# Two hidden tiles of the first network: gate tiles plain by block, input tiles as the first seven-product pair

## The chip, the cores and the metric

The kernel runs on one core of one Trainium2 chip. The metric is the device time of one execution in microseconds (us). Of the kernel before, three runs gave 2673.63, 2676.51 and 2676.99 us; the median is 2676.51 us.

## What is computed

One step of one decoder layer on 1032 tokens (1024 of a prompt and 8 samples), with 1024 features: a gated network, a mixer, a second gated network and a gated input embedding, each with a residual and a layer norm. The change is in the first network:

```python
def swiglu(x, wi, wo):
    g, u = jnp.split(x @ wi, 2, axis=-1)
    return (jax.nn.silu(g) * u) @ wo

x = layer_norm(ALPHA * x + 0.5 * swiglu(x, ffn1_wi, ffn1_wo), ln_g[0], ln_b[0])
```

`wi` has 2 x 2816 columns: 22 tiles of 128 gate columns (`g`) and 22 tiles of 128 input columns (`u`). The second network has the same form with weights of its own.

## The kernel before

**Precision.** Every float32 operand of a matrix product is split into a high part (a rounding copy on ACT) and a low part (a subtraction on DVE): `hilo` for activations (L211, L212), `wload` for plain weight tiles (L148, L149), `wcomb` for combined weight tiles (L258, L259). A product is then three matmuls: high x high, high x low, low x high.

**Tokens.** The tokens lie in four blocks of 256, 260, 256 and 260 columns (`BLK4`). Blocks 0 and 2 belong to half s = 0, blocks 1 and 3 to half s = 1.

**Plain tiles.** `unit` (L169 to L175) multiplies one weight tile of 1024 x 128 with one block: 8 row tiles times 3, which is 24 matmuls. Over four blocks one tile costs 96 matmuls.

**Pairs.** `pair` (L438 to L482, its matmuls in `product`, L432 to L434) computes two weight tiles at once over all four blocks by a scheme of seven products instead of eight: 7 products x 2 halves x 12 matmuls = 168, where two plain tiles take 192. It needs seven combinations of the weights (`wcomb`, L249 to L278) and of the blocks (`xsums`, L219 to L227, called four times, `kp` = 0 to 3, for each half). One call of `xsums` takes four `tmp` tiles, of which there are four in all, two subtractions on DVE (L222, L224), two on POOL (L223, L225), then four copies on ACT (L211) and four subtractions on DVE (L212). The call for half 0 of all `kp` runs in `xlate`; those for half 1 stand beside the first four steps of the first pair (`late_sums`, `beside`). The first pair of a network takes products 0 and 1 of both halves first, since these need no sums, then products 2 to 6 of half 0, then those of half 1.

**The first network.** `ffn` computes hidden tiles 0 and 1 plainly: as each of the blocks 0, 2, 1, 3 arrives, `plain` multiplies it with two gate tiles (k = 0) and two input tiles (k = 1). The eight weight transfers of these four tiles (`wearly`, L533) stand ahead of the prompt's blocks 2, 1 and 3 (`xload`, L292) on SP's queue. Then come 20 pairs: for p = 1 to 10 the gate pair (k = 0) and the input pair (k = 1). `hidden` says what becomes of a result: for k = 0 it is written to the tile `sg` and put through Silu; for k = 1 it is written to a `tmp` tile and multiplied into `sg` (L499). `wi_raw` loads the columns of a pair (L245) into two of four slots in turn; slots 30 and 31 also hold a part of block 2, and slots 32 and 33 two of the eight tiles of the transposed x (`rows1`).

**Order.** The engines run their instructions in order; the order on each is made by a scheduler when the program is built. Weight tiles go round a ring of nine slots (`RING`), and results in PSUM round `mm` (four buffers), `pn` (every fifth plain result) and `aux` (three).

Of the kernel before, what the change touches and what calls it, by code (L numbers as in the profile page):

```python
# [8 lines left out]
F32 = mybir.dt.float32  # L9
# [13 lines left out]
NHID = FF // 128  # L23
# [40 lines left out]
def layer_kernel(ctx: ExitStack, tc: tile.TileContext, I, O):  # L64
# [4 lines left out]
    rawp = ctx.enter_context(tc.tile_pool(name="raw", bufs=3))  # L69
# [7 lines left out]
    def gen(i, dt=F32, n=NT):  # L77

        tag = f"a{i}" if isinstance(i, int) else i
        return sb.tile([128, 1024 if tag in WN else 4 * BM], dt, name=tag, tag=tag)[:, :1024 if tag in WN else n]  # L80
# [403 lines left out]
    def ffn(wi, wo, l, XS, enter, xlate, raws, sgs, RTs, res, groups, plains, tail, extra=None):  # L484
# [3 lines left out]
        def hidden(k, ws, sg, first):  # L488


            def out(i, c, fn):
                d = bs(sg[i], c, BLK4)
                if k == 0:
                    fn(d)
                    S.activation(d, d, AF.Silu)
                else:
                    t = tmp(BN[c % 2])
                    fn(t)
                    V.scalar_tensor_tensor(d, d, 0.5, t, op0=OP.mult, op1=OP.mult)  # L499

            pair(ws, XS, (0, 1), out, first)
# [18 lines left out]
            DQ.dma_start(hsum[5, p], sg[0][:, h[1]])  # L520

        def wi_raw(p, k):
            i = 2 * p + k
            return wraw(wi, k * FF + p * 256, raws[2 * (i % 2):2 * (i % 2) + 2])

        tail_slots = dict(sum(plains, []))
        sg = [gen(sgs[i]) for i in range(2)]
        wp, first = [], []
# [21 lines left out]
        def plain(c):  # L550
            if early and not wp:
                halves(c)
            for k in range(2):
                for i in range(2):
                    if len(wp) < 4:
                        wp.append(wcol(wi, k * FF + i * 128, raws=early.pop(0) if early else ()))
                    if first:
                        ps = first.pop(0)
                    else:
                        ps = unit_ps(BLK4[c][1])  # L560
                        unit(ps, wp[2 * k + i], [xplain(XS[c % 2], c, m) for m in range(8)])
                    d = bs(sg[i], c, BLK4)
                    if k == 0:
                        S.activation(d, ps, AF.Silu)
                    else:
                        with tc.high_priority():
                            V.scalar_tensor_tensor(d, d, 0.5, ps, op0=OP.mult, op1=OP.mult)
                        DQ.dma_start(bs(hscr[i], c, BLK4), d)

        enter(plain, wearly)  # L570
        sreg()
        wr = wi_raw(1, 0)
        with tc.issue_after(order_["entered"]) if l else nullcontext():
            w0 = wcomb(wr)
            xlate()
        for p in range(1, NHID // 2):
            for k in range(2):
                w = w0 if p == 1 and k == 0 else wcomb(wi_raw(p, k))
                if k == 0 and p > 1:
                    sg = [gen(sgs[2 * ((p + 1) % 2) + i]) for i in range(2)]  # L580
                hidden(k, w, sg, p == 1 and k == 0)
            spill(p, sg)

        def split_load(t, src):

# [85 lines left out]

    def enter1(plain, wearly):
        ts = {0: [gen(i)[:, :D] for i in (16, 17)]}
        wt = [t[:, o:o + 512] for t in [gen(i) for i in (22, 10, 24)] for o in (0, 512)]
        wt += [rawp.tile([128, 512], F32, name="raw", tag="raw") for _ in range(2)]
        st = gen(18)[:, :D]
        DQ.dma_start(st[0:8], I["x_sample"][:, 0, :])
        for i in range(2):
            xload(0, ts[0], i * 512, i * 512 + 512)
            for q in range(2):  # L680
                wearly(q, 4 * i, wt[2 * i + q])
        for i in range(4, 8):
            wearly(i // 2, i % 2 * 4, wt[i])
        warm(WARM[0])
        ps = aux()
        for m in range(8):
            T.transpose(ps[:, m * 8:(m + 1) * 8], st[0:8, m * 128:(m + 1) * 128], ident[:8, :8])
        V.tensor_copy(xsv, ps[:, 0:64])
        rows1.extend(gen(i) for i in (19, 23, 32, 33, 11, 25, 34, 35))
        parts = {0: [(0, 0, 1), (1, 4, 5)], 2: [(7, 30, 31), (6, 26, 27)],  # L690
                 1: [(0, 2, 3), (1, 6, 7)], 3: [(7, None, None), (6, 28, 29)]}
        tslots = {2: [20, 21], 1: [8, 9], 3: [12, 13]}
        prev, sr = None, sreg(R)
        for c in (0, 2, 1, 3):
            if c:
                with tc.issue_after(order_["early"]):
                    ts[c] = xtiles(c, tslots[c])
            for j, *ss in parts[c]:
                for q in range(2):
                    xset(X1[c % 2], j, q, ss[q] if ss[q] is not None else sr[:, q * 4 * BM:(q + 1) * 4 * BM])  # L700
            xinput(c, ts[c], rows1)
            xsplit(X1[c % 2], rows1, c)
            if prev is not None:
                plain(prev)
            prev = c
        plain(prev)
        parameters()
        for m in range(8):
            DQ.dma_start(xscr[m], rows1[m])
# [1121 lines left out]
```

## Time and profile before

| | us |
|---|---|
| median of three runs | 2676.51 |
| the profiled execution, whole | 2676.36 |
| its span | 2674.6 |
| PE busy | 2635.3 |
| DVE busy | 1840.7 |
| ACT busy | 1272.1 |
| POOL busy | 650.9 |

The span is the time from the first to the last instruction that the profiler shows; the execution took 1.8 us more. PE is the matrix engine, DVE, ACT and POOL the three others, SP the one that issues most transfers. A busy PE does not say that its matmuls follow one another at the closest spacing, because a matmul of about 0.28 us overlaps the next ones; how far apart they start is read from the timeline. A row of the timeline shows the start in us, the length in us, the engine, the line of the kernel, the operation with its output and input names, and in brackets how long the engine was idle before and what ended that. A row of the windows shows a stretch and its length, then for each engine asked for its busy time and number of instructions, then PE's granted clock, the share of the DMA engines and GB/s.

### The profile page before, as it was taken

The page shows a single profiled execution, that of the slowest core. Times are in us where ns is not written, and L with a number is a line of the kernel's source. Part 1 is how long each engine was busy: PE and PEld are TensorE (multiplying, and loading weights), DVE is VectorE, ACT ScalarE, POOL GpSimd, SP SyncE. Part 2 cuts the span into 40 slices and gives each one's busy share as a digit, 9 for nine tenths or more (in the row PEclk, how much of TensorE's full clock was granted, in tenths as well). Part 3 has the DMA queues.
Part 4 walks back from the last instruction along what each step waited for, and adds up shares of the span by engine and source line. Part 5 has one row for each costly group of instructions (what it writes and reads, how often), then busy time and mean ns, then how long its engine had stood idle before and what let it go on. Part 6 is the DMA issues. An engine that isn't in the chain of part 4 may idle for free.

```text
span 2674.6 us, 56234 instructions
## 1 busy us (share of the span) xinstructions
PE 2635.3 (99%) x21775; PEld 2597.2 (97%) x21775; DVE 1840.7 (69%) x4053; ACT 1272.1 (48%) x2774; POOL 650.9 (24%) x649
## 2 busy tenths in 40 slices
PE   9999999999999999999999999999999999999998
PEld 9999999999999999999999999999999999999888
DVE  6755556987885747555555678658855555888887
ACT  5544445433654444445566555426544444533351
POOL 2222221112431111111110335323322222111454
PEclk9999999999999999999999999999999999999999
DMA  6333235532233334336667676821423323643211
GB/s 208 104 108 102 89 108 185 180 121 68 88 116 96 116 100 125 90 90 191 197 193 240 220 245 210 258 80 51 155 88 108 107 87 107 219 148 117 86 51 58
DMA packets 311924, 355.15 MB, mean 133 GB/s; under 512 B 28536, under 2 KB 246344, under 8 KB 311656
## 3 DMA queue, kind: packets, MB, share of 16 engines
q1 hardware_dynamic: 289336, 330.30, 38.9%
q10 hardware_dynamic: 22320, 21.26, 2.7%
q8 instruction: 170, 2.79, 0.4%
q14 instruction: 98, 0.80, 0.1%
HBM read 246.09 MB, written 105.42 MB: 131 GB/s over the span
## 4 chain that ended last, share of the span: by engine, by line
PE 85%; DVE 7%; DMA 4%; issue 2%; ACT 2%; POOL 1%; SPq 0%; DVEq 0%; ACTq 0%; POOLq 0%
PE mm L432 15%; PE mm L433 14%; PE mm L434 14%; PE aux L432 6%; PE aux L434 6%; PE aux L433 6%; PE mm L172 5%; PE mm L174 5%; PE mm L173 5%; PE pn L172 1%; PE pn L174 1%; PE pn L173 1%; DVE a L212 1%; DVE a L589 1%; DVE a L612 1%
## 5 line engine op out<-in xcount | busy, mean ns | idle before, releaser
L432 PE MATMUL mm<-a,w 128*128 128x260 f32 (+1 forms) x2313 | 655.7, 284 | 3.0 <-DVE a L612 2.5
L433 PE MATMUL mm<-a,w 128*128 128x260 f32 (+1 forms) x2313 | 651.1, 282 | 0.9 <-DVE a L212 0.8
L434 PE MATMUL mm<-a,w 128*128 128x260 f32 (+1 forms) x2313 | 650.1, 281 | 0.0
L432 PEld LDWEIGHTS mm<-a,w 128*128 128x128 f32 x2313 | 435.3, 188 | 11.8 <-issue 8.7
L433 PEld LDWEIGHTS mm<-a,w 128*128 128x128 f32 x2313 | 435.7, 188 | 1.4 <-DVE a L212 1.3
L434 PEld LDWEIGHTS mm<-a,w 128*128 128x128 f32 x2313 | 435.3, 188 | 0.9 <-issue 0.8
L275 POOL TENSOR_TENSOR raw<-a,raw 128x512 f32<-128x512 f32 (+2 forms) x98 | 123.7, 1263 | 1137.4 <-issue 626.8
L259 DVE TENSOR_TENSOR w<-raw,w 128x512 fp32r<-128x512 f32 (+2 forms) x258 | 174.7, 679 | 198.2 <-ACT w L258 196.2
L432 PE MATMUL aux<-a,w 128*128 128x260 f32 (+1 forms) x1000 | 282.2, 282 | 0.2 <-DVE a L612 0.2
L434 PE MATMUL aux<-a,w 128*128 128x260 f32 (+1 forms) x1000 | 281.2, 281 | 0.0
L433 PE MATMUL aux<-a,w 128*128 128x260 f32 (+1 forms) x1000 | 281.1, 281 | 0.0
L432 PE MATMUL mm<-a,e 128*128 128x260 f32 (+1 forms) x785 | 222.4, 283 | 0.9 <-DVE a L612 0.9
L433 PE MATMUL mm<-a,e 128*128 128x260 f32 (+1 forms) x785 | 221.1, 282 | 1.1 <-DVE a L212 1.1
L434 PE MATMUL mm<-a,e 128*128 128x260 f32 (+1 forms) x785 | 220.9, 281 | 0.0
L174 PE MATMUL mm<-a,w 128*128 128x256 f32 (+3 forms) x739 | 208.1, 284 | 0.0
L172 PE MATMUL mm<-a,w 128*128 128x260 f32 (+4 forms) x695 | 198.5, 287 | 2.9 <-DVE a L647 1.7
L258 ACT CAST w<-a 128x512 fp32r<-128x512 f32 (+2 forms) x200 | 117.5, 588 | 171.4 <-PE mm L434 101.7
L173 PE MATMUL mm<-a,w 128*128 128x260 f32 (+4 forms) x695 | 197.4, 285 | 0.0
L432 PEld LDWEIGHTS aux<-a,w 128*128 128x128 f32 x1000 | 188.2, 188 | 2.6 <-issue 2.1
L433 PEld LDWEIGHTS aux<-a,w 128*128 128x128 f32 x1000 | 188.3, 188 | 0.0
L434 PEld LDWEIGHTS aux<-a,w 128*128 128x128 f32 x1000 | 188.2, 188 | 0.0
L258 ACT CAST w<-raw 128x512 fp32r<-128x512 f32 (+2 forms) x258 | 152.2, 591 | 67.2 <-PE aux L434 21.1
(543 smaller groups left out, 7645.9 us busy)
## 6 DMA issues: line engine op xcount, KB each, us to landing
a<-in_ffn_wi_dram SPq DMA_DIRECT2D x80, 512.0 KB
a<-in_w_in_dram SPq DMA_DIRECT2D x68, 512.0 KB
a<-hsum SPq DMA_DIRECT2D x119, 258.0 KB
hsum<-a SPq DMA_DIRECT2D x68, 258.0 KB
a<-in_ffn_wo_dram SPq DMA_DIRECT2D x40, 384.0 KB
a<-in_state_C_dram ACTq DMA_DIRECT2D x32, 256.0 KB
out_dram<-a ACTq DMA_DIRECT2D x32, 256.0 KB
raw<-in_w_b_dram SPq DMA_DIRECT2D x32, 256.0 KB
```

Source lines behind the costliest of these rows:

```text
L172: T.matmul(ps, wh, xh, start=(i == 0), stop=False)
L173: T.matmul(ps, wh, xl, start=False, stop=False)
L174: last = T.matmul(ps, wl, xh, start=False, stop=(i == n - 1))
L212: order_["lo"] = V.tensor_tensor(dst[1], src, F_(dst[0]), op=OP.subtract).ins
L258: S.copy(hi, src)
L259: V.tensor_tensor(lo, src, F_(hi), op=OP.subtract)
L275: G.tensor_tensor(s4, a12, s2, op=OP.subtract)
L432: T.matmul(ps, wh, xh, start=start and kp == 0, stop=False, skip_group_check=True)
L433: T.matmul(ps, wh, xl, start=False, stop=False, skip_group_check=True)
L434: T.matmul(ps, wl, xh, start=False, stop=stop and kp == len(xs) - 1, skip_group_check=True)
L589: V.tensor_tensor(lo, F_(lo), F_(hi), op=OP.subtract)
L612: V.tensor_tensor(r, r, ps, op=op)
```

## The change

In the first network (`l` = 0) only the gate tiles of hidden tiles 0 and 1 are computed plainly. Their input tiles (p = 0, k = 1) become the first of 21 pairs. So four early weight transfers of 256 KB fall away, and the pair loads its two of 512 KB through `wi_raw`, into slots 30 and 31. The results of the first pair now go through `tmp` and L499 into `sg`, and the pair (1, 0) gets a new pair of `sg` tiles. The two hidden tiles are stored whole by `spill`, where before each block was stored by itself (L568). The second network is as before.

```diff
         def wi_raw(p, k):
-            i = 2 * p + k
+            i = 2 * p + k + 1 - bool(l)
             return wraw(wi, k * FF + p * 256, raws[2 * (i % 2):2 * (i % 2) + 2])
...
-            for k in range(2):
+            for k in range(2 if l else 1):
                 for i in range(2):
-                    if len(wp) < 4:
+                    if len(wp) < 2 * k + i + 1:
                         wp.append(wcol(wi, k * FF + i * 128, raws=early.pop(0) if early else ()))
...
         enter(plain, wearly)
         sreg()
-        wr = wi_raw(1, 0)
+        todo = [(p, k) for p in range(NHID // 2) for k in range(2)][2 if l else 1:]
+        wr = wi_raw(*todo[0])
         with tc.issue_after(order_["entered"]) if l else nullcontext():
             w0 = wcomb(wr)
             xlate()
-        for p in range(1, NHID // 2):
-            for k in range(2):
-                w = w0 if p == 1 and k == 0 else wcomb(wi_raw(p, k))
-                if k == 0 and p > 1:
-                    sg = [gen(sgs[2 * ((p + 1) % 2) + i]) for i in range(2)]
-                hidden(k, w, sg, p == 1 and k == 0)
-            spill(p, sg)
+        for i, (p, k) in enumerate(todo):
+            w = wcomb(wi_raw(p, k)) if i else w0
+            if k == 0 and i:
+                sg = [gen(sgs[2 * ((p + bool(l)) % 2) + q]) for q in range(2)]
+            hidden(k, w, sg, i == 0)
+            if k:
+                spill(p, sg)
...
     def enter1(plain, wearly):
         ts = {0: [gen(i)[:, :D] for i in (16, 17)]}
-        wt = [t[:, o:o + 512] for t in [gen(i) for i in (22, 10, 24)] for o in (0, 512)]
-        wt += [rawp.tile([128, 512], F32, name="raw", tag="raw") for _ in range(2)]
+        wt = [t[:, o:o + 512] for t in [gen(i) for i in (22, 10)] for o in (0, 512)]
...
             for q in range(2):
                 wearly(q, 4 * i, wt[2 * i + q])
-        for i in range(4, 8):
-            wearly(i // 2, i % 2 * 4, wt[i])
```

**On SP's queue, at the start of the program.** Rows show the line, the transfer with output and input, and its shape. Before, the block 0 (`a_95`, `a_96`) and eight weight pieces stand ahead of the first tiles of block 2 (`a_191`, `a_192`):

```order
L292 DMA a_96<-in_x_prompt_dram 128x512
L533 DMA a_98<-in_ffn_wi_dram 128x4x128 x2
L533 DMA a_99<-in_ffn_wi_dram 128x4x128 x2
L533 DMA raw<-in_ffn_wi_dram 128x4x128 x2
L292 DMA a_191<-in_x_prompt_dram 128x1024
L292 DMA a_192<-in_x_prompt_dram 128x1024
```

Of the change, with block 2 in `a_184` and `a_185`:

```order
L292 DMA a_96<-in_x_prompt_dram 128x512
L533 DMA a_98<-in_ffn_wi_dram 128x4x128 x2
L292 DMA a_184<-in_x_prompt_dram 128x1024
L292 DMA a_185<-in_x_prompt_dram 128x1024
L292 DMA a_300<-in_x_prompt_dram 128x1024
```

Four transfers are gone from the place ahead of the prompt's tiles.

**On DVE, where the sums of half 1 end.** Before: the last call of `xsums` (L222, L224 and the L212 rows on `a_1015` to `a_1018`), beside the first pair, which writes its results straight to `sg` (`a_94`):

```order
L222 TENSOR_TENSOR tmp<-a_133 128x260
L212 TENSOR_TENSOR a_1015<-tmp,a_1015 128x260
L212 TENSOR_TENSOR a_1016<-tmp,a_1016 128x260
L224 TENSOR_TENSOR tmp<-a_137,tmp 128x260
L212 TENSOR_TENSOR a_1017<-tmp,a_1017 128x260
L212 TENSOR_TENSOR a_1018<-tmp,a_1018 128x260
L259 TENSOR_TENSOR w_1215<-a_1208,w_1215 128x512
L212 TENSOR_TENSOR a_1015<-tmp,a_1015 128x260
L212 TENSOR_TENSOR a_1016<-tmp,a_1016 128x260
L469 SCALAR_TENSOR_TENSOR a_94<-sreg,mm 128x256
```

Of the change, with the same sums in `a_781` to `a_784`:

```order
L222 TENSOR_TENSOR tmp<-a_126 128x260
L499 SCALAR_TENSOR_TENSOR a_93<-a_93,tmp 128x260
L212 TENSOR_TENSOR a_782<-tmp,a_782 128x260
L224 TENSOR_TENSOR tmp<-a_130,tmp 128x260
L212 TENSOR_TENSOR a_783<-tmp,a_783 128x260
L259 TENSOR_TENSOR w_990<-a_983,w_990 128x512
L212 TENSOR_TENSOR a_784<-tmp,a_784 128x260
L469 SCALAR_TENSOR_TENSOR tmp<-sreg,mm 128x256
L212 TENSOR_TENSOR a_781<-tmp,a_781 128x260
L212 TENSOR_TENSOR a_782<-tmp,a_782 128x260
```

The pair's own results (L469, L499) now go through `tmp` tiles and stand among the sums.

**On PE, where these sums are used.** Before, the last matmuls that need the low parts of `a_1015` and `a_1016`, behind product 6 of half 0 (`w_861`):

```order
L434 MATMUL mm<-a_198,w_861 128x256
L433 MATMUL mm<-a_1015,w_847 128x260
L434 MATMUL mm<-a_1015,w_847 128x260
L433 MATMUL aux<-a_1016,w_850 128x260
L434 MATMUL aux<-a_1016,w_850 128x260
L432 MATMUL aux<-a_1016,w_850 128x260
```

Of the change, with `a_781` and `a_782`, and behind them the next pair's first matmul (`w_990`):

```order
L432 MATMUL aux<-a_782,e_615 128x260
L434 MATMUL mm<-a_783,e_618 128x260
L433 MATMUL mm<-a_781,w_612 128x260
L434 MATMUL mm<-a_781,w_612 128x260
L433 MATMUL aux<-a_782,e_615 128x260
L434 MATMUL aux<-a_782,e_615 128x260
L432 MATMUL mm<-a_132,w_990 128x256
```

The low parts of the last sums stand 15 matmuls later in the pair than before: 140 of its matmuls come ahead of the first of these four rows, where 125 did.

## The prediction

> **What bounds the kernel now.** I read the page first, then the windows over the start.
>
> ```profile
> PE 2635.3 (99%) x21775; PEld 2597.2 (97%) x21775; DVE 1840.7 (69%) x4053; ACT 1272.1 (48%) x2774; POOL 650.9 (24%) x649
> PE 85%; DVE 7%; DMA 4%; issue 2%; ACT 2%; POOL 1%; SPq 0%; DVEq 0%; ACTq 0%; POOLq 0%
> 10.70:62.50 51.80, 51.80 (x436) 51.80 (x435) 35.55 (x78) 31.49 (x90) 10.74 (x11) 1.00 0.60 210
> 62.50:82.50 20.00, 20.00 (x171) 20.00 (x170) 18.25 (x38) 13.07 (x35) 8.08 (x9) 1.00 0.27 85
> 65.60:77.50 11.90, 11.90 (x103) 11.90 (x102) 11.90 (x25) 8.00 (x22) 6.46 (x7) 1.00 0.28 90
> ```
>
> The first row gives each engine's busy time, the second the chain that ended last: PE holds it. The windows (busy PE, PEld, DVE, ACT, POOL) show that PE never stops between 10.7 and 82.5 us, so a matmul removed there is time removed. But the third window has DVE at 11.90 of 11.90: while the sums of x for half 1 are made, **DVE has no room either**. The change takes work from PE ahead of just this stretch.
>
> **What goes.** Four tile-blocks of two input tiles are 2 x 4 x 24 = 192 matmuls; a pair is 168. So 24 matmuls go. Their spacing, from the timeline:
>
> ```profile
> 10.71 0.56 PE L172 MATMUL mm<-a,w 128*128 128x256 f32 x1
> 12.33 0.27 PE L174 MATMUL mm<-a,w 128*128 128x256 f32 x1
> 14.32 0.28 PE L172 MATMUL mm<-a,cd 128*128 128x256 f32 x1
> 19.87 1.15 PE L308 MATMUL aux<-ident,a 128*128 128x128 f32 x9
> 62.52 0.36 PE L432 MATMUL mm<-a,e 128*128 128x256 f32 x1
> 77.42 0.28 PE L433 MATMUL mm<-a,w 128*128 128x260 f32 x1
> 85.46 0.28 PE L432 MATMUL aux<-a,e 128*128 128x256 f32 x1
> ```
>
> The first pair begins at 62.52; the row at 85.46 is 192 matmuls later, so one takes 22.94 / 192 = 0.1195 us (not the 0.28 us that each is in flight). **Saving: 24 x 0.1195 = 2.87 us**, if PE stays busy. That is already less than 0.2% of the time (5.35 us), about what a measurement of this kernel can tell from no change.
>
> **When PE would want the sums.** Without the 192 plain matmuls PE would begin the pair 22.94 us earlier, at 39.6. The last low parts of the sums are wanted after 140 matmuls of the pair: 39.6 + 140 x 0.1195 = 56.3. Before it was 62.52 + 125 x 0.1195 = 77.46, and PE's row is at 77.42. DVE's last sum came in the same moment:
>
> ```profile
> 41.70 0.69 DVE L267 TENSOR_TENSOR raw<-a,a 128x512 f32<-128x512 f32 x1 [1.96 <-DMA a<-in_ffn_wi_dram]
> 76.78 0.76 DVE L212 TENSOR_TENSOR a<-tmp,a 128x260 fp32r<-128x260 f32 x2
> ```
>
> Its two rows end at 77.54 (76.78 + 0.76). There was no slack, and PE now comes 21.1 us earlier. Can DVE?
>
> **When DVE can begin.** The chain starts with transfers:
>
> ```profile
> 13.79 0.33 SPq L329 DMA_DIRECT2D tmp<-in_b_in_dram  x1
> 14.64 0.30 SPq L330 DMA_DIRECT2D tmp<-in_b_in_dram  x1
> 15.91 0.31 SPq L332 DMA_DIRECT2D tmp<-in_ln_g_dram  x1
> 17.21 0.31 SPq L332 DMA_DIRECT2D tmp<-in_ln_b_dram  x1
> SPq L332 <- DMA a<-in_x_prompt_dram: 1.9, 2, 1.0
> 35.91 1.00 SPq L245 DMA_DIRECT2D a<-in_ffn_wi_dram  x2
> ```
>
> SP issues each transfer when the one eight places ahead has landed (the waits row: L332 waits for tiles of x). So the last two early weights landed by 13.8 and 14.6, 0.85 us apart, and block 2 by 15.9 and 17.2. Four weights fewer are 3.4 us: block 2 lands at about 12.5 and 13.8. PE gets through the 24 matmuls that now stand ahead of its transposes at 14.3 (24 lie between 10.71 and 14.32), so the tiles don't hold it.
>
> From there ACT paces the start, copying and splitting:
>
> ```profile
> 20.39 1.20 ACT L314 COPY a<-aux 128x256 f32<-128x256 f32 x4 [0.43 <-PE aux L308]
> 31.06 0.73 ACT L211 CAST a<-tmp 128x256 fp32r<-128x256 f32 x2
> 40.17 0.62 ACT L258 CAST e<-a 128x512 fp32r<-128x512 f32 x1 [0.34 <-DMA a<-in_ffn_wi_dram]
> ```
>
> Blocks 2 and 1 took it 20.39 to 31.8. Now that starts near 15.2 (14.3, 0.4 for the first transposes, and 0.52, as from 19.87 to 20.39) and ends near 26.6. The pair's weights go into slots 30 and 31, which hold block 2 for PE. PE reads slot 31 last after 60 matmuls and 32 transposes (0.128 us each, 1.15 / 9): 14.3 + 7.2 + 4.1 = 25.6. Before, the same wait ended with the issue at 35.91; the first transfer was in use at 40.17, 4.3 us later, the second at 41.70. So the second lands at 25.6 + 4.3 = 29.9, and there DVE takes L267, where it took it at 41.70: **only 11.8 us earlier**, since the transfer follows block 2 and not the pair.
>
> **How long DVE then needs.** From L267 to the last sum nearly the same work lies before it as before:
>
> ```profile
> 41.60:77.50 35.90, 32.45 (x67) 1.00 0.52 186
> 42.31 0.69 DVE L259 TENSOR_TENSOR e<-a,e 128x512 fp32r<-128x512 f32 x1
> L567 DVE SCALAR_TENSOR_TENSOR a<-a,mm 128x260 f32<-128x260 f32 x3 | 1.3, 420 | 1.2 <-PE mm L174 1.2
> L212 DVE TENSOR_TENSOR a<-tmp,a 128x260 fp32r<-128x260 f32 (+1 forms) x28 | 15.0, 571 | 1.7 <-ACT a L211 1.5
> 90.69 0.43 DVE L499 SCALAR_TENSOR_TENSOR a<-a,tmp 128x256 f32<-128x256 f32 x1
> 98.64 0.41 DVE L469 SCALAR_TENSOR_TENSOR tmp<-sreg,mm 128x256 f32<-128x256 f32 x1
> ```
>
> DVE was busy 32.45 us (DVE alone in this window). In the new order four L567 (4 x 0.42) and one weight split (0.69) leave this stretch; three L212 (0.42 without company, see below), two L499 and one L469 enter: 32.45 - 2.37 + 2.53 = 32.6 us. If it works without a break it ends at 29.9 + 32.6 = 62.5, not at 56.3. ACT and POOL had 8.00 and 6.46 of 11.90 in the dense part and don't set the pace.
>
> **The sum.** PE passes the four late matmuls at about 62.7 instead of 39.6 + 144 x 0.1195 = 56.8, so it **waits 5.9 us**, in several pieces from product 2 of half 1 on. Against 2.87 saved that is +3.0 us. Forecast: 2676.36 (the profiled execution) + 3.0 = 2679.4; the median of the runs, 2676.51, lies beside it.
>
> **What I cost at nothing.** The removed weight splits (four L149 on DVE, done before 17 us while DVE waits for ACT) and stores (L568) are off PE's path, so they give nothing; the larger stores of `spill` come when SP's queue has only weights for later pairs. The second pair's slots 32 and 33 come free with the last call of the sums: I put the issue 3.5 us ahead of its end, near 59, the landing 4.3 later, near 63.3; they are wanted as a high part 12 matmuls after the four late ones, at 64.2; a landing 2 us later costs 1 us. Further on, ring and PSUM turns have another phase, and the order differs near the ends of both networks. PE's waits there:
>
> ```profile
> PE mm L432 <- DVE a L612: 4.4, 10, 0.8
> PE aux L407 <- DVE sreg L404: 2.8, 1, 2.8
> PE mm L172 <- DVE a L647: 2.7, 6, 0.8
> ```
>
> Their sum, 9.9 us, is what a better phase could take away at most; I take nothing, and 1 us to each side.
>
> **Is the 32.6 firm?** It rests on L212 at 571 ns on average, which depends on POOL:
>
> ```profile
> 43.85 0.76 DVE L212 TENSOR_TENSOR sreg<-a,sreg 128x260 fp32r<-128x260 f32 x2
> 72.27 1.31 DVE L212 TENSOR_TENSOR a<-tmp,a 128x260 fp32r<-128x260 f32 x2
> 72.09 0.87 POOL L223 TENSOR_TENSOR tmp<-a,a 128x260 f32<-128x260 f32 x1 [0.37 <-DVE a L212]
> L222 DVE TENSOR_TENSOR tmp<-a 128x260 f32<-128x260 f32 (+1 forms) x6 | 3.3, 546 | 0.0
> L259 DVE TENSOR_TENSOR w<-a,w 128x512 fp32r<-128x512 f32 x3 | 3.1, 1050 | 0.0
> ```
>
> Two L212 took 0.76 us alone and 1.31 beside a POOL subtraction of 0.87. The sums need the same eight POOL subtractions per half, so I keep the slow mean. Without it 28 x (0.571 - 0.42) = 4.2 us go from L212 alone and some 1.9 from L222 and L259 (6 x 0.13 and 3 x 0.36, by 0.42 and the 0.69 above): DVE would end near 56, and the wait with it. The other end: DVE's idle time as it was (35.9 - 32.45, less the 2.0 before L267: 1.5 us), the second transfer at its old 5.3 us behind its issue (+1.0), and the `tmp` rival below (+1.5): +3.0 becomes +7.
>
> The Trainium skill (GPSIMD Engine Reference, Key points) says that POOL shares its SBUF interfaces with DVE, with contention for DVE instructions that have two SBUF inputs. L212 is one, and the trace agrees (1.31 against 0.76); by that rule the slow mean moves with the sums, and 32.6 stands; without the rule the sum would be the full saving, 2673.5.
>
> **Rivals.**
> - *The cover holds* (DVE near 56): 2676.4 - 2.9 = 2673.5. For it: PE never waited between 10.7 and 82.5 in before. Against: DVE's 11.90 of 11.90. It also needs the transfer by 28.
> - *The four `tmp` tiles become the bound*, the slow side. The first pair's results now pass through them (L469, L499 among the sums), so a call of `xsums` may wait for the third tile of the last call instead of its first. Three calls for half 1 fill the window from 65.60 to 77.50, some 4 us each. About 0.8 us more in each (an L454 or L469 and an L499) gives 3.2: 2682.6. It decides if DVE stands idle between L224 and L222 and the last sum comes after 65.
> - *Slow matmuls after the waits.* From 10.71 to 12.33 seven matmuls started 0.23 us apart, though the granted clock is 1.00 in that window. If PE starts so again after its last wait, 7 x 0.11 = 0.8 us: 2680.2. The Trainium skill (TensorE: Matmul & The Clock Gate, HAM oscillation) warns of gaps over some 3.4 us, after which matmuls run at half speed; no stretch of this trace has such a gap past 10.7, so it can't be checked here, and my waits are shorter pieces.
> - *It doesn't do what it says*: excluded, the new order has 24 matmuls fewer.
>
> **Chances.** Forecast (+0.5 to +5.3) 0.52; the slow matmuls 0.05; the cover 0.18; `tmp` 0.20; phases at the ends of the networks 0.05, to either side. From these: faster by over 0.2% 0.04, within 0.2% 0.72, slower 0.24 (most of `tmp`, and the upper edge of the others). Range 2674.0 to 2684.5: it leaves out half of the cover's case and what lies past +8.
>
> **What would show it.** Right: in the new profile PE waits for L212 and L211 between 50 and 65 us, some 6 us in all; L267's first row stands near 30; the last L212 of the sums near 62.5; and the second pair begins near 65.6, where the first of 20 pairs began at 62.52. Wrong: PE busy throughout with the second pair at 59.7 (the saving stands); or the waits are over 8 us; or equal starts and a difference past 500 us (phases).

## The result, and the profile after

| | before | changed |
|---|---|---|
| median, us | 2675.31 (2673.63 to 2676.99) | 2691.30 (2689.38 to 2697.09) |
| profiled execution, us | 2676.36 | 2697.09 |
| its span, us | 2674.6 | 2695.3 |

The ratio is 1.0064, 95% interval 1.0052 to 1.0076: the changed kernel is slower by 16.0 us. Its profiled execution is the slowest of its four, 5.8 us above their median, so sizes that are read at its end are some us too large. The page's first rows on busy time and on the chain that ended last, of the changed kernel:

```profile
PE 2641.9 (98%) x21751; PEld 2600.9 (96%) x21751; DVE 1843.1 (68%) x4066; ACT 1275.2 (47%) x2785; POOL 655.2 (24%) x651
PE 81%; DVE 8%; DMA 6%; issue 2%; ACT 2%; POOL 1%; SPq 0%; DVEq 0%; ACTq 0%; POOLq 0%
```

PE has the 24 matmuls fewer (21775 before), yet it is busy longer, and the chain goes through DMA and DVE more often (4% and 7% before). To see where, count PE's matmuls from the start up to a given time. These are windows of the kernel before and then of the changed one (stretch, its length, PE's busy time and matmuls, granted clock, share of the DMA engines, GB/s):

```profile
0.00:100.00 100.00, 97.26 (x785) 1.00 0.52 174
0.00:460.00 460.00, 457.26 (x3818) 1.00 0.38 125
0.00:500.00 500.00, 497.26 (x4155) 1.00 0.40 131
0.00:2640.00 2640.00, 2609.72 (x21605) 1.00 0.43 134
```

```profile
0.00:100.00 100.00, 92.13 (x718) 1.00 0.49 169
0.00:460.00 460.00, 451.84 (x3738) 1.00 0.36 119
0.00:500.00 500.00, 487.68 (x4010) 0.99 0.39 128
0.00:2640.00 2640.00, 2595.66 (x21407) 1.00 0.42 133
```

A matmul takes (500 - 100) / (4155 - 785) = 0.1187 us. The changed kernel has 24 fewer to do, so its **lag** at a time is (before's count - 24 - its count) x 0.1187. That gives 5.1 us at 100, 6.6 at 460, 14.4 at 500 and 20.7 at 2640. Full use of the saving would read as -2.85. There are two losses: about 5 us at the start, which the prediction looked for (as +3.0), and about 8 us between 460 and 500, of which it says nothing. Beyond 500 the lag goes down to 10.7 at 600 and up to 21.1 at 1900, with steps of up to 8 us both ways near 2500 and 2620, where both kernels have waits that come at different times. The rise of 6.7 us from 500 to 1900 is not explained; in e1 below it is 1.1, and this execution is 5.8 us above the median.

**The start.** All of PE's waits between 30 and 65 us in the changed kernel's timeline (start, length, in brackets the idle time ahead and what ended it), then the rows of DVE at both ends of its chain, and the window over that chain (busy PE, PEld, DVE, ACT, POOL):

```profile
36.30 0.39 PE L173 MATMUL mm<-sreg,w 128*128 128x260 f32 x1 [0.51 <-DVE sreg L212]
40.01 0.39 PE L173 MATMUL mm<-a,w 128*128 128x260 f32 x1 [0.58 <-DVE a L212]
49.01 0.39 PE L433 MATMUL mm<-a,w 128*128 128x256 f32 x1 [0.84 <-DVE a L212]
53.24 0.39 PE L432 MATMUL mm<-a,w 128*128 128x256 f32 x1 [0.90 <-ACT sreg L457]
55.95 0.39 PE L433 MATMUL mm<-a,w 128*128 128x260 f32 x1 [0.55 <-DVE a L212]
60.10 0.39 PE L433 MATMUL aux<-a,e 128*128 128x260 f32 x1 [0.61 <-DVE a L212]
64.03 0.39 PE L433 MATMUL mm<-a,w 128*128 128x260 f32 x1 [1.68 <-DVE a L212]
```

```profile
29.46 0.69 DVE L267 TENSOR_TENSOR raw<-a,a 128x512 f32<-128x512 f32 x1 [0.95 <-DMA a<-in_ffn_wi_dram]
63.56 0.76 DVE L212 TENSOR_TENSOR a<-tmp,a 128x260 fp32r<-128x260 f32 x2
```

```profile
29.40:64.40 35.00, 29.20 (x229) 27.49 (x228) 33.70 (x68) 21.79 (x59) 16.46 (x16) 1.00 0.50 176
```

DVE (third engine of the window: 33.70 of 35.00) has next to no room, PE stands behind it, and the last sum ends at 63.56 + 0.76 = 64.3 instead of the 62.5 of the forecast.

**The end of the first network's pairs.** Two windows of the kernel before, then the same of the changed one, and PE's waits between 400 and 520 us in the changed one (the kernel before has none there):

```profile
470.00:480.00 10.00, 10.00 (x87) 10.00 (x86) 10.00 (x22) 6.08 (x11) 2.76 (x2) 1.00 0.85 277
480.00:490.00 10.00, 10.00 (x87) 10.00 (x86) 10.00 (x27) 3.85 (x8) 1.02 (x1) 1.00 0.20 62
```

```profile
470.00:480.00 10.00, 7.83 (x66) 7.62 (x65) 10.00 (x24) 8.15 (x14) 0.00 (x0) 1.00 1.05 393
480.00:490.00 10.00, 8.01 (x42) 7.80 (x42) 4.97 (x9) 2.44 (x5) 0.00 (x0) 0.67 0.37 115
```

```profile
PE mm L432 <- DVE a L613: 2.2, 1, 2.2
PE aux L432 <- ACT a L589: 2.0, 1, 2.0
PE mm L432 <- ACT sreg L450: 0.3, 1, 0.3
```

In these 20 us PE starts 66 + 42 = 108 matmuls where it started 174: 66 x 0.1187 = 7.8 us. Only 4.2 us of it are waits (the third one, 0.3 us, lies at 455); most of the rest is the clock, 0.67 in the second window. The second wait is for ACT's copy (L589) of a tile of the sums of the hidden tiles. The timeline of SP and ACT of the changed kernel there, and one row of SP's waits between 400 and 500 us (us in total, times, longest):

```profile
474.89 0.32 SPq L506 DMA_DIRECT2D hscr<-a  x1
478.81 0.34 SPq L506 DMA_DIRECT2D hscr<-a  x1
482.59 1.75 SPq L588 DMA_DIRECT2D a<-hsum  x2
485.33 0.62 ACT L589 CAST a<-a 128x516 fp32r<-128x516 f32 x1 [0.71 <-DMA a<-hsum]
```

```profile
SPq L588 <- DMA hscr<-a: 6.6, 4, 2.8
```

L506 stores the two hidden tiles of the last pair; L588 loads sums for the output stage, and its waits are above all for those stores. That points to shared memory. The change turns the parity of the `sg` tiles: pair p now uses `sgs[2 * (p % 2)]`, before `sgs[2 * ((p + 1) % 2)]`. So the last pair, p = 10, has its `sg` in slots 14 and 15, before in 34 and 35. The table of the output stage, which the diff does not touch, puts sums of the **first** group into 14 and 15, and of the second into 34 and 35. Before, the first group's loads into 14 and 15 came behind the stores of pair 9; now they wait until the last pair is computed and stored. The first wait is for DVE's additions (L613), which stand on DVE behind splits of such tiles.

### The profile page after: what moved, and what is told of

It reads as the page before. It is cut to its first block, busy times and chain, and to the rows that moved or that the text cites. A ratio compares the mean times of both kernels' runs of the same rounds, so it can differ in the third digit from the quotient of the medians.

```text
span 2695.3 us, 56209 instructions
## 1 busy us (share of the span) xinstructions
PE 2641.9 (98%) x21751; PEld 2600.9 (96%) x21751; DVE 1843.1 (68%) x4066; ACT 1275.2 (47%) x2785; POOL 655.2 (24%) x651
## 4 chain that ended last, share of the span: by engine, by line
PE 81%; DVE 8%; DMA 6%; issue 2%; ACT 2%; POOL 1%; SPq 0%; DVEq 0%; ACTq 0%; POOLq 0%
PE mm L432 14%; PE mm L434 14%; PE mm L433 14%; PE aux L432 6%; PE aux L433 6%; PE aux L434 6%; PE mm L172 4%; PE mm L174 4%; PE mm L173 4%; DVE a L212 2%; PE pn L172 1%; PE pn L174 1%; PE pn L173 1%; DMA a<-hsum 1%; DVE a L590 1%
## 5 line engine op out<-in xcount | busy, mean ns | idle before, releaser
L432 PE MATMUL mm<-a,w 128*128 128x256 f32 (+1 forms) x2364 | 670.0, 284 | 4.4 <-DVE a L613 2.2
L433 PE MATMUL mm<-a,w 128*128 128x260 f32 (+1 forms) x2364 | 665.4, 282 | 4.9 <-DVE a L212 4.8
L434 PE MATMUL mm<-a,w 128*128 128x260 f32 (+1 forms) x2364 | 664.0, 282 | 0.0
L432 PEld LDWEIGHTS mm<-a,w 128*128 128x128 f32 x2364 | 444.6, 188 | 11.7 <-issue 6.2
L433 PEld LDWEIGHTS mm<-a,w 128*128 128x128 f32 x2364 | 445.2, 188 | 6.4 <-DVE a L212 6.3
L434 PEld LDWEIGHTS mm<-a,w 128*128 128x128 f32 x2364 | 444.7, 188 | 0.5 <-issue 0.4
L432 PE MATMUL aux<-a,w 128*128 128x256 f32 (+1 forms) x990 | 280.1, 283 | 2.2 <-ACT a L589 2.0
L433 PE MATMUL aux<-a,w 128*128 128x256 f32 (+1 forms) x990 | 279.3, 282 | 0.0
L434 PE MATMUL aux<-a,w 128*128 128x256 f32 (+1 forms) x990 | 279.0, 282 | 0.0
L432 PE MATMUL mm<-a,e 128*128 128x260 f32 (+1 forms) x770 | 218.0, 283 | 4.9 <-DVE a L613 2.3
L433 PE MATMUL mm<-a,e 128*128 128x260 f32 (+1 forms) x770 | 217.0, 282 | 0.0
L434 PE MATMUL mm<-a,e 128*128 128x260 f32 (+1 forms) x770 | 216.9, 282 | 0.0
L172 PE MATMUL mm<-a,w 128*128 128x256 f32 (+4 forms) x712 | 202.1, 286 | 4.4 <-ACT w L148 2.5
L173 PE MATMUL mm<-a,w 128*128 128x256 f32 (+4 forms) x712 | 202.5, 286 | 1.0 <-DVE a L212 0.6
L174 PE MATMUL mm<-a,w 128*128 128x256 f32 (+4 forms) x712 | 200.7, 285 | 0.0
```

The lines of the kernel that those rows point to most:

```text
L172: T.matmul(ps, wh, xh, start=(i == 0), stop=False)
L173: T.matmul(ps, wh, xl, start=False, stop=False)
L174: last = T.matmul(ps, wl, xh, start=False, stop=(i == n - 1))
L432: T.matmul(ps, wh, xh, start=start and kp == 0, stop=False, skip_group_check=True)
L433: T.matmul(ps, wh, xl, start=False, stop=False, skip_group_check=True)
L434: T.matmul(ps, wl, xh, start=False, stop=stop and kp == len(xs) - 1, skip_group_check=True)
```

## The experiments

The theory then: two separate losses, slots (A, about 8 us) and DVE at the start (about 5 us). The rivals for the first: the phase of the PSUM turns, the slots of the weights. Each kernel was timed in five rounds against the kernel before, whose median was 2675.3 to 2676.3 in the four comparisons.

| run | lag at 30 | at 100 | at 460 | at 500 | at 2640 | median, us | ratio to before, 95% |
|---|---|---|---|---|---|---|---|
| changed kernel | -3.3 | 5.1 | 6.6 | 14.4 | 20.7 | 2691.3 | 1.0064 [1.0052, 1.0076] |
| e1_slots | -3.2 | 5.7 | 7.1 | 7.1 | 9.0 | 2683.4 | 1.0028 [1.0017, 1.0039] |
| e2_raws | -2.7 | 5.0 | 5.9 | 14.4 | 17.8 | 2692.1 | 1.0059 [1.0046, 1.0072] |
| e3_turn | -4.7 | 3.0 | 3.9 | 11.9 | 17.6 | 2693.8 | 1.0063 [1.0050, 1.0075] |
| e4_three | -4.9 | 4.6 | 5.7 | 5.7 | 8.7 | 2685.2 | 1.0035 [1.0022, 1.0047] |
| e5_before_swapped | 0.0 | 0.1 | 0.1 | 8.0 | 10.2 | 2682.5 | 1.0028 [1.0018, 1.0039] |
| e6_early | -2.3 | 4.6 | 5.8 | 5.8 | 7.4 | 2683.6 | 1.0033 [1.0021, 1.0046] |
| e7_dve | -4.6 | -0.6 | 0.8 | 0.8 | 2.0 | 2681.2 | 1.0022 [1.0013, 1.0032] |
| e8_both | -4.3 | 0.0 | 1.2 | 1.1 | 2.0 | 2677.8 | 1.0009 [1.0000, 1.0017] |
| e9_later | -4.6 | -2.3 | -1.1 | -1.2 | -0.5 | 2677.7 | 1.0007 [0.9998, 1.0015] |
| e10_before_dve | -1.3 | -1.4 | -1.4 | -1.4 | 0.0 | 2677.6 | 1.0008 [0.9999, 1.0018] |
| e11_start_only | -3.4 | -0.8 | 0.2 | 7.4 | 6.6 | 2683.5 | 1.0032 [1.0019, 1.0044] |
| e12_pool_more | -4.6 | 4.9 | 5.8 | 5.8 | 8.5 | 2685.1 | 1.0036 [1.0024, 1.0049] |

The lags are worked out as above from one profiled execution each, the medians from all executions; e5 and e10 are kernels before with an edit, so nothing is subtracted for the 24 matmuls there.

In a kernel of the changed order a lag of -2.85 at 30 us would be a start as in the kernel before. These lags differ by up to 2.6 us from execution to execution, ahead of PE's first wait for a low part: in the kernel before, the changed kernel and e1 matmuls start 0.21 us apart until about 12.3 us and 0.12 apart behind that, while in e7, e10 and e12 they start 0.12 apart from 10.0 us on. So what a kernel loses at the start is the step from 30 to 100 us: 8.4 us in the changed kernel, 8.9 in e1, 6.9 in e6, 4.0 in e7, 4.3 in e8, 2.3 in e9, 2.6 in e11, 9.5 in e12, and nothing in e5 and e10. Between 100 and 460 us the lag then rises by another 0.9 to 1.5 us in every kernel with the changed order, and not in e5 and e10. PE waits there for 0.3 us in the changed kernel and not at all in e8 and e9; but matmuls start 0.1191 us apart in e8 and e9, and 0.1187 apart in the kernel before, e5 and e10. What causes that is not shown.

### e1_slots: the slots exchanged

```diff
-    G1 = [((1, 2, 3), (0, 1, 2, 3, 4, 5, 6, 7, 14, 15, 22, 23, 8, 9, 10, 11, 12, 13, 26, 27, 28)),
+    G1 = [((1, 2, 3), (0, 1, 2, 3, 4, 5, 6, 7, 34, 35, 22, 23, 8, 9, 10, 11, 12, 13, 26, 27, 28)),
```

(and likewise in the two other groups, where 34, 35 and 14, 15 change places, and in the table `T1` of the last stage)

> The changed kernel, with the slots 14, 15 and 34, 35 exchanged in the output stages of the first network, so that the last pair's sg tiles no longer lie where the first output group loads its sums of the hidden tiles. Theory A (slots): the rise of the lag between 470 and 490 us (64 matmuls, some 7.6 us, of which 4.2 us are two waits) goes, the granted clock there is back at 1.00, and the median is 6 to 8 us below the changed kernel's 2691.3: about 2684. Theory B (phases of the ring and of the PSUM turns, or the weights' slots 30 to 33): the waits at 479 and 486 us stay or come back elsewhere, and the median is within 2 us of 2691.3.

2683.4: 7.9 us below the changed kernel. The lag does not move between 460 and 500 (7.1 at both), and the two windows of this run are whole again:

```profile
470.00:480.00 10.00, 10.00 (x86) 10.00 (x85) 10.00 (x23) 8.62 (x16) 0.00 (x0) 1.00 1.05 393
480.00:490.00 10.00, 10.00 (x87) 10.00 (x86) 10.00 (x23) 4.58 (x10) 2.77 (x2) 1.00 0.41 144
```

Theory A holds, and the wait for DVE has gone with the other.

### e2_raws, e3_turn, e4_three: the other phases

e2 gives the first output weights the slots of the other parity; e3 sets the counter of plain results forward; e4 has both, and e1's exchange.

```diff
-                t = gen(raws[2 * (i % 2) + q])[:, :g * 256].rearrange("p (k n) -> p k n", n=256)
+                t = gen(raws[2 * ((i + 1 - bool(l)) % 2) + q])[:, :g * 256].rearrange("p (k n) -> p k n", n=256)
```

```diff
         enter(plain, wearly)
+        turn["n"] += 8 * (1 - bool(l))
```

> The changed kernel, with the first segment of output weights loaded into the two slots of the other parity (32, 33 in place of 30, 31), as these stood to the last pair before. Theory A (slots of sg): nothing of the loss at 470 to 490 us goes; the median is within 2 us of 2691.3. Theory C (slots of the weights): the first output weights come sooner, the waits at 479 and 486 us go, and the median is near 2684.

> The changed kernel, with the counter of the plain results set forward by 8 after the first network's plain tiles, so that every later plain result takes the PSUM buffer and the accumulation form that it took before. Theory A (slots): the stretch up to 500 us is as in the changed kernel, with 14 us of lag at 500 us, and beyond it the lag moves by some 3 us at most; the median is 2688 to 2692. Theory B (phases): the waits at 479 and 486 us go or the later lag falls by over 5 us, and the median is 2686 or lower.

> The changed kernel with all three edits: sg slots exchanged, first output weights in the other parity's slots, and the counter of plain results set forward. What then is left against the kernel before is the start (about 5 us by the lag at 100 us) and the phase of the ring of nine. If the three terms add up: 2675.3 + 5 and a few us for the ring's phase, 2680 to 2684. If it is the same as the exchange of slots alone, the other two phases cost nothing.

e2 and e3 stay at 2692.1 and 2693.8, with a jump of 8 us between 460 and 500 in both; e3 is 1.8 us above the window that was expected of it, on the side away from theory B. e4 is at 2685.2, no better than e1 alone. Neither the weights' slots nor the counter of the plain results carries a part of the loss that can be measured. The phase of the ring of nine slots was not turned back in any run.

### e5_before_swapped: the collision put into the kernel before

The exchange of e1 in the kernel before, whose last pair has its `sg` in slots 34 and 35.

> The kernel before, with the slots 14, 15 and 34, 35 exchanged in the output stages of the first network, so that its last pair's sg tiles (34, 35) now lie where the first output group loads its sums. Theory A (slots): the same collision is now in the kernel before; PE waits some 4 us in two pieces between 470 and 490 us and the median rises by 6 to 9 us, to 2682 to 2685. Rival (the collision costs only together with the later start of the changed kernel, or with the phase of its ring): no change beyond 2 us.

2682.5, 7.0 us more than the kernel before beside it (2675.5). The lag is 0.1 up to 460 us and 8.0 at 500. Windows of this run, and its longer wait:

```profile
476.00:478.00 2.00, 0.00 (x0) 0.00 (x0) 0.43 (x1) 0.25 (x1) 0.00 (x0) 0.91 0.78 157
480.00:482.00 2.00, 2.00 (x11) 2.00 (x10) 1.06 (x2) 0.00 (x0) 0.00 (x0) 0.50 0.02 4
```

```profile
PE aux L432 <- ACT a L588: 3.2, 1, 3.2
```

The same loss, from an exchange of slot numbers in a kernel that has nothing else of the change. With e1 that shows A in both directions. After the wait the granted clock is 0.50, so 11 matmuls start in 2 us where about 17 would.

### e6_early, e7_dve, e8_both: the start

All three have e1's exchange. e6 loads the first pair's weights into two free slots; e7 does all subtractions of the first network's sums on DVE; e8 does both.

```diff
-            return wraw(wi, k * FF + p * 256, raws[2 * (i % 2):2 * (i % 2) + 2])
+            return wraw(wi, k * FF + p * 256, raws[2 * (i % 2):2 * (i % 2) + 2] if p or l else [24, 18])
```

```diff
-        G.tensor_tensor(t3, b22, b12, op=OP.subtract)
+        g.tensor_tensor(t3, b22, b12, op=OP.subtract)
         V.tensor_tensor(t2, b22, t1, op=OP.subtract)
-        G.tensor_tensor(t4, t2, b21, op=OP.subtract)
+        g.tensor_tensor(t4, t2, b21, op=OP.subtract)
...
-            xsums(X1[0], rows1, 0, kp)
-        late_sums(X1[1], rows1, ((18, 22, 10, 24), (19, 23, 11, 25)))
+            xsums(X1[0], rows1, 0, kp, V)
+        late_sums(X1[1], rows1, ((18, 22, 10, 24), (19, 23, 11, 25)), V)
```

> The changed kernel with sg slots exchanged, and the first pair's weights loaded into slots 24 and 18, which nothing holds then, in place of 30 and 31, which hold block 2. The pair then has its weights near 20 us instead of 29. Theory D (the transfer's place sets DVE's start): the weight splits go into DVE's gaps between 15 and 29 us (3.7 us in all in the run with sg slots exchanged), the last sum comes 3 to 4 us earlier, near 61, and the median is near 2680. Rival (DVE and ACT have no room for it there; ACT is busy without a gap from 16 to 36 us): the copies of x come later by as much, the last sum stays within 1 us of 64.4, and the median within 2 us of 2683.4.

> The changed kernel with sg slots exchanged, and the two POOL subtractions of every call of the sums done on DVE instead (16 in all). Theory E (POOL slows DVE): two low parts take 1.30 us beside a POOL subtraction and 0.75 alone, so each POOL subtraction costs DVE 0.55 us, and one on DVE costs it 0.34; the chain gets 16 x 0.2 = 3.2 us shorter although DVE does more, the 1.3 us pairs of L212 go, and the median is 2680 to 2682. Rival (the 1.3 us have another cause, and DVE's work is all that counts): 16 x 0.34 = 5.4 us more on DVE, last sum near 69, median near 2688.

> The changed kernel with sg slots exchanged, the first pair's weights early and all subtractions of the sums on DVE. If D and E both hold and add up, the last sum is near 58, the start costs next to nothing, and the median is 2676 to 2678; if only one holds, 2680 to 2682. If the second pair's weights, whose slots come free with the last call of the sums, then set the pace, the last sum is early but the second pair still begins past 64.

e6 is at 2683.6, where e1 is at 2683.4. DVE takes the weights 3.4 us earlier than in e1 (25.59 instead of 28.99), and the last sum ends at 63.9, in e1 at 63.5. By itself the early transfer is worth nothing that the time shows; theory D falls, the rival holds. A row of e6 shows one place where the time goes, DVE waiting for POOL:

```profile
25.59 0.68 DVE L267 TENSOR_TENSOR raw<-a,a 128x512 f32<-128x512 f32 x1
30.93 1.50 DVE L222 TENSOR_TENSOR tmp<-a 128x256 f32<-128x256 f32 x1 [0.63 <-POOL tmp L225]
63.14 0.76 DVE L212 TENSOR_TENSOR a<-tmp,a 128x260 fp32r<-128x260 f32 x2
```

e7 puts 16 subtractions **more** on DVE, and the lag at 100 us falls from 5.7 to -0.6 (1.4 us of that stand at 30 us already). The largest group of DVE's chain, between 29.4 and 64.4 us, in the changed kernel and then in e7 (count, busy time, mean ns of one, idle time ahead), then the first row and the last sum of the chain in e1 and in e7 (L268 there is L267 of e1):

```profile
L212 DVE TENSOR_TENSOR a<-tmp,a 128x260 fp32r<-128x260 f32 x16 | 9.6, 621 | 0.0
```

```profile
L212 DVE TENSOR_TENSOR a<-tmp,a 128x260 fp32r<-128x260 f32 x16 | 6.7, 436 | 0.0
```

```profile
28.99 0.69 DVE L267 TENSOR_TENSOR raw<-a,a 128x512 f32<-128x512 f32 x1 [0.39 <-DMA a<-in_ffn_wi_dram]
62.73 0.75 DVE L212 TENSOR_TENSOR a<-tmp,a 128x260 fp32r<-128x260 f32 x2
```

```profile
27.90 0.69 DVE L268 TENSOR_TENSOR raw<-a,a 128x512 f32<-128x512 f32 x1 [0.46 <-DMA a<-in_ffn_wi_dram]
59.24 0.42 DVE L212 TENSOR_TENSOR a<-tmp,a 128x260 fp32r<-128x260 f32 x1
```

The low parts take 436 ns where they took 621, and the last sum ends at 59.7, 3.8 us sooner than in e1. As the chain also begins 1.1 us sooner, it is 2.7 us shorter (34.5 and 31.8 us; 3.2 were expected). In the trace theory E holds. In time e7 is at 2681.2, in the expected window and 2.2 us below e1, and its executions scatter from 2677.4 to 2687.7; its profiled one took 2678.5. e8 is at 2677.8, in the window for both theories and 5.6 us below e1, with the start at a lag of 0.0. Its last sum ends at 58.6, 1.1 us sooner than in e7, so with POOL's subtractions away the early weights do bring the chain forward. Why e7's median stays 3.4 us above e8's at an equal start, the profiles don't show.

### e9_later, e10_before_dve, e11_start_only, e12_pool_more

e9 is e8 with the second pair's weight splits held back; e10 is the kernel before with e7's edit; e11 is the changed kernel with both edits of e8 and without e1's exchange; e12 is e1 with four low parts more on POOL.

```diff
-            w = wcomb(wi_raw(p, k)) if i else w0
+            wr = wi_raw(p, k) if i else None
+            with tc.issue_after(order_["sums"]) if i == 1 and not l else nullcontext():
+                w = wcomb(wr) if i else w0
```

```diff
-            hilo(xparts(X7, j, kp), t)
+            hilo(xparts(X7, j, kp), t, G if X7 is X1[1] and j == 5 else None)
```

(the first is e9's, where `order_["sums"]` is the last low part of the late sums; the second e12's)

> The kernel of the last run but one step (sg slots exchanged, first pair's weights early, all subtractions of the sums on DVE), with the weight splits of the second pair held back until the last low part of the sums. In the run before it DVE split the second pair's first weights at 54.70 (1.49 us beside POOL), ahead of the last sums. Theory F (what is left of the loss is DVE's work ahead of the last sums): the last sum comes 1.5 us sooner, at 57.0, the lag at 100 us falls from 0.0 to -1 or lower, and the median is 2674 to 2676.5. Rival (the second pair then waits for its weights instead): PE waits past 58 us for the second pair's first weights, the lag stays within 0.5 us of 0, and the median is 2677 to 2679.

> The kernel before, with all subtractions of the sums in its first network on DVE. Theory (DVE sets the start only in the changed kernel): PE never waited between 10.7 and 82.5 us in the kernel before, so a faster DVE is worth nothing there; the median stays within 1.5 us of 2675.5. Rival (the edit is a gain by itself, whatever the order): 2 us less or more, 2673.5 or lower.

> The changed kernel with the two edits at the start (first pair's weights early, subtractions of the sums on DVE) and the sg slots as the change has them. If the loss at the start and the loss of the slots simply add up: the lag at 460 us is about 1 us as with both edits, the jump of some 7 to 8 us between 460 and 500 us stays, and the median is 2691.3 - 5.6 = 2685.7. Rival (the collision hurts less when the start is on time, or more): 2683 or lower, 2688 or higher.

> The changed kernel with sg slots exchanged, and one low part more of each of the four late sums taken from DVE and given to POOL (4 in all). Theory E (POOL slows DVE): each takes 0.34 us off DVE and costs it about 0.55 in the instructions beside it, so the chain gets no shorter although DVE does less: last sum at 64.4 to 66, median 2683 to 2686. Rival (only the number of DVE's instructions counts): 4 x 0.34 = 1.4 us sooner, last sum at 63, median 2682.

**e9**: the lag at 100 us is -2.3, where it is 0.0 in e8, but not by theory F. The last sum ends at 58.4 (58.6 in e8, 57.0 expected), and the waits at the start come to 1.3 us in three pieces (1.45 in four in e8). The difference is above all the clock: from 58.25 to 61.66 us the granted clock is 0.50 in e8, which costs some 1.5 us (as worked out in the last section), and 1.00 in e9. The median, 2677.7, is that of e8; it lies above the window of theory F and in that of the rival, though PE does not wait for the second pair's weights. Against the kernel before (2676.1) the interval takes in no change. No version beats the kernel before.

**e10**: 2677.6 beside 2676.1, no change that can be told. The -1.4 us of lag at 100 stands at 30 us already, so DVE has no part in it, and is gone at the end (0.0). By the number on record it is 0.6 us outside the theory's window, on the side away from the rival; a faster DVE brings the kernel before nothing. DVE is faster there, too: the 16 low parts of half 1 take 421 ns (the row, from 40 to 77.5 us) where they took 550.

```profile
L212 DVE TENSOR_TENSOR a<-tmp,a 128x260 fp32r<-128x260 f32 x16 | 6.3, 421 | 1.2 <-ACT a L211 1.2
```

**e11**: 2683.5, 7.8 us below the changed kernel; 5.6 were expected, so it lies between the sum and the rival. The jump between 460 and 500 us stays (0.2 to 7.4), with waits of 3.2 and 1.6 us. The two losses stand beside each other.

**e12**: the first row and the last sum of its chain:

```profile
27.85 0.69 DVE L267 TENSOR_TENSOR raw<-a,a 128x512 f32<-128x512 f32 x1 [0.61 <-DMA a<-in_ffn_wi_dram]
60.67 1.82 DVE L212 TENSOR_TENSOR a<-tmp,a 128x260 fp32r<-128x260 f32 x2
```

The last sum ends at 62.5, 1.0 us sooner than in e1, near the rival's 63; but the chain also begins 1.1 us sooner. It takes 34.6 us where e1's takes 34.5: no shorter, although DVE has four subtractions fewer, which is what theory E says. The median, 2685.1, lies in theory E's window; with executions from 2682.8 to 2686.5 against e1's 2680.6 to 2688.4 it would not decide by itself. Four subtractions on POOL thus cost DVE about what they took off it, by these two executions (1.4 + 0.1) / 4 = 0.4 us each, less than the 0.55 expected.

## Why the prediction was wrong, point by point

**The direction was right, the size was not**: +3.0 us was forecast, +16.0 came, outside the range.

- *What goes*: right. 21751 matmuls, 24 fewer.
- *When DVE can begin*: right. L267 was put at 29.9 and stands at 29.46, and what ended the wait is the transfer.
- *How long DVE then needs*: a term mis-sized. 32.6 us were forecast, and it took 29.46 to 64.3 = 34.8. Of the 2.2 us that were missing, 1.2 are two gaps in which DVE waits for ACT's copies (L211, at 45.58 and 47.01 us), where the forecast had none. The other 1.0 is longer instructions. The low parts of the sums were taken at the mean of before, 571 ns for all shapes; the 16 of half 1 took 621 here and 550 before, but those of half 0 took 482 here and 598 before, so together they came out about as priced. What came out longer are the low parts of the plain block in `sreg` (692 ns for 423), L270 (1234 for 684) and the new L499, which were priced at 0.43 us and took 0.97 where POOL subtracts beside them:

```profile
58.74 0.97 DVE L499 SCALAR_TENSOR_TENSOR a<-a,tmp 128x260 f32<-128x260 f32 x1
```

The forecast had asked whether the slow mean is firm and kept it; e7 and e10 show that it goes with POOL's subtractions. The Trainium skill (GPSIMD Engine Reference, Key points) names contention between POOL and DVE's instructions with two SBUF inputs; e7's 436 against 621 ns agrees.

- *The sum*: PE waits 5.9 us, +3.0. The bracketed waits come to 5.67 us, which looks right and is not: the forecast's 5.9 was the whole delay of PE, and the brackets leave out a part of it. From 62.07 to 64.03 two matmuls start 1.96 us apart where the spacing is 0.12, so 1.84 are lost; the bracket says 1.68. The next spacing is 0.22, another 0.1. So each wait costs some 0.26 us more, 7 x 0.26 = 1.8, 7.5 us in all; less 2.85 that is +4.6, and the windows say 5.1 at 100 us. (From 30 us on PE falls back by 8.4 us, from a lag of -3.3 to 5.1; the waits explain 7.5 of them.) The forecast was 2 us short here, by DVE's term.
- *What I cost at nothing*: **the step that failed.** "Ring and PSUM turns have another phase, and the order differs near the ends of both networks ... I take nothing, and 1 us to each side." Turned phases of the plain results' PSUM turns and of the weights' slots are indeed worth nothing that can be measured (e2, e3, e4); the ring's was not tried. But the same count that turned them also turned the slots of `sg`, and the prediction never set these against the table of the output stage. That one overlap costs 7.9 us (e1), 7.0 (e5), 5.7 (e11 over e8), about half of the 16. It stood in the code: the list of `sgs`, the parity, and the two tables.
- *Rivals*: the cover did not hold. The `tmp` tiles were not the bound: DVE was busy 33.70 of 35.00, not idle between L224 and L222. The **slow matmuls after waits**, given 0.05 and 0.8 us, do occur, and not at the start of this profile but in the second loss, at nearly twice the price each (last section); in e1, e4, e8 and e12 they occur at the start. Two readings behind that rival were wrong. The seven matmuls from 10.71 to 12.33 did not run at a full clock: the trace's record of the granted clock begins with its first full stretch, at 12.29. And the kernel before did hold a test of what a wait does: behind this row the granted clock is 0.50 between 1702 and 1705 us.

```profile
1699.85 0.39 PE L172 MATMUL mm<-a,e 128*128 128x256 f32 x1 [1.98 <-ACT e L148]
```

- *What would show it*: the signs of being right at the start came near enough (5.67 us of waits, L267 at 29.46, the last sum at 64.3 for 62.5, the second pair at 64.71 for 65.6), and the time was wrong all the same. "Equal starts and a difference past 500 us (phases)" was the sign looked for on the side of the phases. The sign that came is a step between 470 and 490 on top of a late start.

**The account.** Of the 16.0 us, e1 takes off 7.9, and the start's edits another 5.6 (e8). (Against the kernel before in the same comparison the three are at +16.0, +7.1 and +2.3.) What is left is 2677.8 - 2675.5 = 2.3 us, and e8's interval, 1.0000 to 1.0017, is 0 to 4.5 us. Whether anything real is left stays open. The saving of 2.85 us can be followed in e9: 2.3 of it go between 30 and 100 us (lag -4.6 to -2.3), and 1.2 more up to 460 us by the wider spacing that all kernels of the changed order show, so nothing of it remains. These are single executions, and the cause of the wider spacing is open.

## What to carry to other kernels

When a change shifts the number of trips of a loop by one, every buffer that is chosen by parity changes hands: list who uses each of these slots next, also in tables that the diff does not touch, and compare the last user's store with the next user's load. On an engine that is full, price new work at its cost in company, and ask whether work given to POOL comes back as slower instructions on DVE; here giving 16 subtractions back to DVE made its chain 2.7 us shorter. Before two traces are compared at one time, see whether they were level before the edit acts: here the start alone differed by up to 2.6 us. A bracketed wait of PE understates its cost, by about 0.26 us each here.

## What the hardware showed beyond that

A short wait of PE can cost a second time through the clock. Matmuls of the changed kernel around its two waits near 480 us, and windows of 2 us after each (changed kernel):

```profile
479.36 0.39 PE L432 MATMUL mm<-a,e 128*128 128x256 f32 x1 [2.17 <-DVE a L613]
486.00 0.62 PE L432 MATMUL aux<-a,w 128*128 128x256 f32 x3 [1.99 <-ACT a L589]
```

```profile
480.00:482.00 2.00, 2.00 (x11) 2.00 (x11) 1.96 (x4) 0.68 (x2) 0.00 (x0) 0.50 0.72 276
488.00:490.00 2.00, 2.00 (x11) 2.00 (x11) 0.69 (x3) 0.00 (x0) 0.00 (x0) 0.50 0.00 0
```

Some 0.6 to 0.9 us after each wait the spacing goes from 0.12 to 0.21 us, for 3.2 us (479.94 to 483.17, and 486.87 to 490.09): the granted clock is 0.50. Each time that loses 3.2 x (1 - 0.1187 / 0.214) = 1.4 us, 2.9 for both, and with 4.2 us of waits and what the brackets leave out it makes up the 7.8.

The Trainium skill (TensorE: Matmul & The Clock Gate, HAM oscillation) puts the limit at gaps of over about 3.4 us. The measurement decides: gaps of 2.17 and 1.99 us were followed by half speed here. It is not the length of one gap alone. The same wait of 1.68 us ahead of the last sum is followed by a whole clock in the changed kernel and by half of it in e1 (its row). The windows show two stretches of 3.41 us each around this wait, first of the changed kernel and then of e1:

```profile
60.08:63.49 3.41, 2.24 (x16) 2.03 (x16) 3.41 (x5) 1.32 (x4) 2.48 (x2) 1.00 0.52 154
63.49:66.90 3.41, 2.87 (x22) 2.79 (x23) 3.41 (x10) 2.25 (x7) 0.00 (x0) 1.00 0.00 0
```

```profile
63.20 0.41 PE L433 MATMUL mm<-a,w 128*128 128x260 f32 x1 [1.68 <-DVE a L212]
```

```profile
60.01:63.43 3.42, 1.74 (x15) 1.53 (x13) 3.42 (x6) 1.58 (x5) 2.18 (x2) 1.00 0.45 143
63.43:66.84 3.41, 3.41 (x17) 3.38 (x17) 3.41 (x9) 2.04 (x5) 0.00 (x0) 0.50 0.00 0
```

The fourteen traces agree on what tells the two apart. In each of them the granted clock changes only at whole multiples of 3.41 us from its first change, so a wait counts by the stretch of 3.41 us that it falls into. In e1 the whole wait lies in one stretch, in which PE is idle for 1.68 us; in the changed kernel it lies across a border (63.49), and the stretches hold 1.17 and 0.54 us. Of all stretches at full clock, the 25 in which PE was idle for 1.78 us or more in sum were all followed by half speed. Of those with less, eight were: seven with 1.60 to 1.73 us, and one with 1.25 (e8); others with 1.60 to 1.76 us were not. So half speed follows where PE was idle for about half of such a stretch. This is read from the traces; no run changed it alone. It may be a part of why equal starts give executions that differ by some us, but no run here isolates that.
